# The place of the down projections in the first feed-forward block of a hybrid decoder layer

## Chip, cores and metric

The kernel runs on one core of one Trainium2 chip. The metric is the device time of one execution in microseconds (us). Three timed runs of the kernel before gave 2674.72, 2677.0 and 2678.22 us, with a median of 2677.0 us. The profile is of one further execution, which took 2671.87 us.

## The reference

One layer of a decoder: a mixer, a memory cross-attention and a gated convolutional feed-forward part, over 2048 prompt rows and 32 sample rows of 1024 features, in float32. The change lies in the feed-forward part alone:

```python
n3 = rmsnorm(x, p['g_ffn'])
g, ffn_state = causal_dwconv(n3 @ p['w_ffn_gate'], ffn_prev, p['w_ffn_conv'], p['b_ffn_conv'])
x = x + (jax.nn.gelu(g) * (n3 @ p['w_ffn_up'])) @ p['w_ffn_down']
```

The hidden width is 3072, which is 24 units of 128 features.

## The kernel before

Phases 0 to 2 hold the mixer and the cross-attention. Phase 3 (`phase3`, L668) is the feed-forward part. It takes the 2080 columns (rows of x) in three blocks of 696, 692 and 692 columns; the change touches the first. In each block a hand-written plan (L692 to L700) sets the order of the program: 24 gate/up units `g` and 12 down projections `d`, each `d` for a pair of units. In the first block of the kernel before, pair c (units 2c and 2c+1) has its down projection right behind unit 2c+2; the last two pairs have theirs behind unit 23.

A gate/up unit (`gate_up`, L1353) computes a gate and an up matrix product of one unit as seven products of half size, from combinations of weights and inputs. Each product has 4 steps of 3 matmuls (every float32 number is split into a high and a low part), 12 matmuls of 348 columns, so 84 in a unit. The products go to four PSUM banks: X takes products 0 and 4, Y product 1, Z products 2 and 5, V products 3 and 6. VectorE (DVE) adds Y to `u`, then Z and V to what came of that. The product behind each bank's second use waits for the first use to be read: product 5 for the add of Z, product 6 for the add that writes `up[:, H:W]` from V (H is 348, half of the block). Behind product 5 comes the add into `gb`, and behind product 6 the add into the other half of `up`. Then the tail of the unit runs on ScalarE (ACT) and DVE: `gc` (L1404 on ACT, two L1406 on DVE, the gelu L1407 on ACT), the product into `up` (L1408), and the split of `up` into its high part `ah` (ACT, L79) and its low part `al` (DVE, L83).

A down projection (`down`, L1418) has eight groups, one for each 128 output features. A group is 12 matmuls, six of the pair's first unit and six of the second, into a PSUM tile `pd` of which there are two. Behind each group DVE adds `pd` into `acc` (L1430). Group m+2 waits until the add of group m has freed its tile.

Weights come in pieces (`piece`, L659): seven for a unit, four for a down projection. Raw weights `wr` are loaded by DMA on the queue of SyncE (SP) into four slots, two for each unit or down projection. ACT writes the high half of a piece `pc`, GpSimd (POOL) or DVE the low half (L79, L83). In the first block DVE also makes four sums of raw weights for each unit (`ws`, L606), and the pieces made of them are written to DRAM (`kept_s`), from which the other two blocks load them. Pieces are asked for four ahead of their use, and there are six slots for them. POOL, ACT and DVE also prepare the next block's inputs beside this (L761, L766, L774).

The tile framework decides the order of each engine's queue at build time, by the program's order as priority and by its own estimate of when an operation becomes ready. Each queue then runs in that order. Slots matter here: `ah` and `al` have four slots each (2·CH), `up` and `gc` one, the temporaries `u`, `u2`, `u4` three.

```python
up = q1.tile([128, W], F, name="up")
ah = q1.tile([128, W], R, name="ah", bufs=2 * CH)
```

Of the kernel before, what the change touches and what calls it, by code (L numbers as in the profile page):

```python
# [23 lines left out]
CH = 2  # L24
SMQ, SMO = 1, 2
OUT_PRIO = 170
N3_PRIO = 400
X0_PRIO = 100
G_MIX, G_CROSS, G_MEM, G_FFN, G_FIN = 0, 8, 16, 24, 32
C_CW, C_CB, C_BA, C_BX, C_LAM = 40, 56, 60, 64, 68  # L30
C_FW, C_FB, C_SINK, C_SROW, C_END = 72, 144, 168, 176, 177
# [14 lines left out]
class _Kernel:  # L46
# [295 lines left out]
    def p1_load(self, s, k):  # L342
        t0, W = SB1[s][0], self.width1(s)
        if s == 0:
            if k not in self.x0:
                self.x0[k] = self.lp.tile([128, W], F, name="x0", tag=f"lru{k % 2}", bufs=4)
                with self.tc.high_priority(X0_PRIO):
                    self.nc.sync.dma_start(self.x0[k], self.I["x"][k, :, t0:t0 + W])
# [233 lines left out]
    def piece_stream(self):  # L582

        nc, I = self.nc, self.I
        kept = {}

        def load(src):
            raw = self.wraw.tile([128, 1024], F, name="wr", tag="wr")  # L590
            nc.sync.dma_start(raw, src)
            return raw

        def raws(kind, i):
            if kind == "d":
                return [load(I["w_down"][i * CH + e]) for e in range(CH)]
            g = load(I["w_gate"][i])
            if ("s", i, 0) not in kept:
                return g, load(I["w_up"][i])
            u = self.wsum.tile([128, 512], F, name="ws", tag="ws")  # L600
            nc.sync.dma_start(u, I["w_up"][i][:, 512:1024])
            return g, u

        def sums(x, y, op):
            t = self.wsum.tile([128, 512], F, name="ws", tag="ws")
            nc.vector.tensor_tensor(out=t, in0=x, in1=y, op=op)  # L606
            return t

        def halves(src, lo_eng):
            t = self.wpc.tile([128, 2, 512], R, name="pc", tag="pc")  # L610
            self.split(src, t[:, 0], t[:, 1], "act", lo_eng)
            return t

        def keep(key, src, lo_eng="dve"):
            t = halves(src, lo_eng)
            kept[key] = self.dram.tile([128, 2, 512], F, name="kept_" + "_".join(map(str, key)))
            nc.sync.dma_start(kept[key], t.bitcast(F))
            return t

        def again(key):  # L620
            t = self.wpc.tile([128, 2, 512], R, name="pc", tag="pc")
            nc.sync.dma_start(t.bitcast(F), kept[key])
            return t

        def paired(f, g, u):
            a11, a12 = g[:, 0:512], g[:, 512:1024]
            if ("s", f, 0) in kept:
                yield halves(a11, "pool")
                for e in range(3):
                    yield again(("s", f, e))  # L630
                yield halves(a12, "pool")
                yield again(("s", f, 3))
                yield halves(u, "pool")
                return
            a21, a22 = u[:, 0:512], u[:, 512:1024]
            yield halves(a11, "pool")
            s1 = sums(a21, a22, OP.add)
            s2 = sums(s1, a11, OP.subtract)
            yield keep(("s", f, 0), s2)
            yield keep(("s", f, 1), s1, "pool")  # L640
            yield keep(("s", f, 2), sums(a11, a21, OP.subtract))
            yield halves(a12, "pool")
            yield keep(("s", f, 3), sums(a12, s2, OP.subtract))
            yield halves(a22, "pool")

        def plain(rs):
            for h in range(2):
                for r in rs:
                    yield halves(r[:, h * 512:h * 512 + 512], "pool")

        nxt = raws(*self.units[0])
        for n, (kind, i) in enumerate(self.units):
            now, nxt = nxt, None
            for t in paired(i, *now) if kind == "g" else plain(now):
                yield t
                if nxt is None and n + 1 < len(self.units):
                    nxt = raws(*self.units[n + 1])

    def piece(self, ahead=4):  # L659
        while len(self.pq) <= ahead:  # L660
# [7 lines left out]
    def phase3(self):  # L668
        nc, tc, I, O = self.nc, self.tc, self.I, self.O
        NC = NF // CH  # L670
        with ExitStack() as es:
            pool = lambda n, b: es.enter_context(self.tc.tile_pool(name=n, bufs=b))
            self.wpc = pool("wpc", 6)
            self.wsum = pool("wsum", 3)
            self.n3a = pool("n3a", 1)
            self.n3b = pool("n3b", 1)
            self.q1 = pool("f1", 1)
            self.q2 = pool("f2", 2)
            self.xs = es.enter_context(tc.tile_pool(name="x3", bufs=1, side="right"))
            self.psa = es.enter_context(tc.tile_pool(name="ps3a", bufs=1, space=bass.MemoryType.PSUM))  # L680
            self.psb = es.enter_context(tc.tile_pool(name="ps3b", bufs=1, space=bass.MemoryType.PSUM))
            self.pq = []
            self.p3c = []
            self.n3 = {}
            with tc.high_priority(N3_PRIO):
                for i in range(7):
                    self.p3_ops(0, i)
            self.xpool = lambda: dict(pool=self.xs, tag="x", bufs=4)
            self.fst = self.q1.tile([128, NF, NB, 2], F, name="fst")
            nc.sync.dma_start(self.fst, I["ffn_conv"])  # L690
            self.sfo = self.q1.tile([128, NF, NB, 2], F, name="sfo")
            plan = []  # L692
            for s in range(3):
                for f in range(NF):
                    plan.append(("g", s, f))
                    c = f // CH - 1
                    if f % CH == 0 and f and not (s < 2 and c == NC - 2):
                        plan.append(("d", s, c))
                if s < 2:
                    plan += [("d", s, NC - 2), ("d", s, NC - 1)]  # L700
            self.units = [(k, i) for k, s, i in plan if k in "gd"] + [("d", NC - 1)]
            self.pieces = self.piece_stream()
            acts, sb = {}, None
            for kind, s, i in plan:
                if kind == "g":
                    if i == 0:
                        rest = sb.final() if s else self.p2[3].rstd3_steps()
                        ready = self.p3_prep(s + 1) if s < 2 else iter(())
                        sb = _P3(self, s)

                    def after(e, s=s, i=i):
                        if i < 2 and (s or i) and not (i == 0 and e in (0, 1, 3, 4)):
                            next(rest, None)
                            if i == 1 and e > 3:
                                next(rest, None)
                        elif 4 <= i < 20 and e % 3 == 1:
                            next(ready, None)
                        if s < 2 and i == NF - 1:
                            self.p3_ops(s + 1, e)

                    acts[i] = sb.gate_up(i, after)
                    if i == 1:
                        sb.load_acc()
                else:
                    sb.down([acts[i * CH + e] for e in range(CH)], s < 2 and i == NC - 1)
            sb.tail([acts[NF - CH + e] for e in range(CH)])
# [897 lines left out]
```

## Time and profile before

| | us |
|---|---|
| median of three timed runs | 2677.0 |
| lowest and highest of them | 2674.72, 2678.22 |
| the profiled execution | 2671.87 |
| its span, first to last instruction | 2670.1 |
| TensorE busy in the span | 2567.0 (96%) |
| DVE busy in the span | 1547.3 (58%) |

The profile is one execution. TensorE appears as PE (matmuls) and PEld (weight loads), the granted TensorE clock as a share of full speed. Times in rows count from the span's start. An idle time in brackets is the one just before the instruction, with what ended it. In the views by stretch each engine has its busy time and its number of instructions.

### The profile page before, as it was taken

The numbers are of one execution on the slowest core, as the hardware profiler recorded it, in microseconds if no ns is written. First come the engines' busy times: TensorE is split into PE (matmuls) and PEld (weight loads), VectorE is DVE, ScalarE is ACT, GpSimd is POOL, SyncE is SP. The second block draws the span as 40 slices with busy tenths as digits, with TensorE's granted clock in tenths as the row PEclk, the third lists the DMA queues.
The fourth block names the chain that finished last, engine by engine and source line by source line (L and its number), as shares of the span: only waits on it lengthen the run. The fifth ranks groups of instructions, "written<-read, shape, count | busy, mean of one in ns | idle before, by whom it ended". The sixth has DMA issues, their size and how long they took to land.

```text
span 2670.1 us, 40945 instructions
## 1 busy us (share of the span) xinstructions
PE 2567.0 (96%) x15221; PEld 2408.2 (90%) x15221; DVE 1547.3 (58%) x2637; ACT 1078.8 (40%) x2071; POOL 992.6 (37%) x928
## 2 busy tenths in 40 slices
PE   6999999998999999899999999999999999999997
PEld 5778788986998887899999999999999999999997
DVE  6577666666542434677777675554544454454545
ACT  5455736474442434434343443232332333233233
POOL 3422211013302144445454545453543444343342
PEclk9899999999999999999999999999999999999998
DMA  7664544466756787955555668665564875545442
GB/s 248 249 225 171 192 148 148 151 214 235 271 174 231 246 273 266 348 182 210 177 212 182 213 233 307 206 204 205 197 207 166 302 255 173 159 160 167 148 164 78
DMA packets 195671, 553.72 MB, mean 207 GB/s; under 512 B 28628, under 2 KB 49364, under 8 KB 192784
## 3 DMA queue, kind: packets, MB, share of 16 engines
q1 hardware_dynamic: 195472, 551.10, 59.7%
q8 instruction: 120, 1.97, 0.3%
q14 instruction: 79, 0.65, 0.1%
HBM read 409.22 MB, written 141.80 MB: 206 GB/s over the span
## 4 chain that ended last, share of the span: by engine, by line
PE 78%; DVE 8%; DMA 5%; ACT 3%; issue 3%; POOL 2%; SPq 0%; POOLq 0%; DVEq 0%; ACTq 0%
PE pg L137 30%; PE pd L137 19%; PE pin L137 10%; PE po L137 6%; PE pmo L137 3%; PE pq L137 3%; DVE gc L1406 2%; PE sc L137 1%; DVE ws L606 1%; DMA wr<-in_w_up_dram 1%; PE tp L859 1%; DMA x<-in_x_dram 1%; PE pa L137 1%; DMA x<-x2d 1%; PE msc L137 1%
## 5 line engine op out<-in xcount | busy, mean ns | idle before, releaser
L137 PE MATMUL pg<-n,pc 128*128 128x346 f32 (+1 forms) x6048 | 977.6, 322 | 7.4 <-DVE up L1360 3.1
L137 PEld LDWEIGHTS pg<-n,pc 128*128 128x128 f32 x6048 | 968.6, 189 | 10.8 <-issue 3.8
L83 POOL TENSOR_TENSOR pc<-wr,pc 128x512 fp32r<-128x512 f32 x312 | 435.6, 1403 | 374.9 <-ACT pc L79 372.0
L137 PE MATMUL pd<-ah,pc 128*128 128x346 f32 (+1 forms) x2240 | 461.8, 325 | 22.7 <-DVE acc L1430 22.7
L137 PEld LDWEIGHTS pd<-ah,pc 128*128 128x128 f32 x2240 | 378.8, 191 | 26.8 <-DVE acc L1430 25.5
L79 ACT ACTIVATE pc<-wr 128x512 fp32r<-128x512 f32 x312 | 195.2, 628 | 412.2 <-PE pd L137 255.6
L1430 DVE TENSOR_TENSOR acc<-pd,acc 128x692 f32<-128x692 f32 (+1 forms) x280 | 245.4, 877 | 163.8 <-PE pd L137 162.2
L137 PE MATMUL pd<-al,pc 128*128 128x346 f32 (+1 forms) x1120 | 271.7, 324 | 0.0
L1406 DVE SCALAR_TENSOR_TENSOR gc<-gb,pp,gc 128x696 f32<-128x696 f32 (+2 forms) x144 | 156.5, 1087 | 79.0 <-ACT gc L1404 77.4
L137 PEld LDWEIGHTS pd<-al,pc 128*128 128x128 f32 x1120 | 197.1, 191 | 0.0
L137 PE MATMUL pin<-n1h,wh 128*128 128x512 f32 (+1 forms) x560 | 187.7, 362 | 4.0 <-DVE ql L83 1.7
L137 PE MATMUL pin<-n1l,wh 128*128 128x512 f32 (+1 forms) x560 | 186.0, 358 | 4.7 <-DVE n1l L83 4.7
L137 PE MATMUL pin<-n1h,wl 128*128 128x512 f32 (+1 forms) x560 | 185.2, 357 | 1.7 <-POOL wl L83 1.7
L83 POOL TENSOR_TENSOR wl<-wr,wh 128x1024 fp32r<-128x1024 f32 x35 | 85.6, 2454 | 208.9 <-ACT wh L79 162.1
L1360 DVE TENSOR_TENSOR u<-pg,u 128x346 f32<-128x346 f32 (+1 forms) x144 | 73.9, 513 | 127.5 <-PE pg L137 127.5
L83 POOL TENSOR_TENSOR pc<-ws,pc 128x512 fp32r<-128x512 f32 x72 | 97.8, 1359 | 129.8 <-ACT pc L79 116.8
L1360 DVE TENSOR_TENSOR gb<-pg,u 128x314 f32<-128x314 f32 (+2 forms) x96 | 38.8, 425 | 161.3 <-PE pg L137 161.3
L137 PEld LDWEIGHTS pin<-n1h,wh 128*128 128x128 f32 x560 | 103.2, 194 | 21.3 <-DVE ql L83 2.3
L79 ACT ACTIVATE pc<-ws 128x512 fp32r<-128x512 f32 x144 | 89.8, 626 | 78.9 <-PE pd L137 25.8
L137 PEld LDWEIGHTS pin<-n1l,wh 128*128 128x128 f32 x560 | 102.5, 193 | 19.8 <-DVE n1l L83 5.8
L137 PEld LDWEIGHTS pin<-n1h,wl 128*128 128x128 f32 x560 | 102.7, 194 | 16.9 <-POOL wl L83 2.1
L766 POOL TENSOR_TENSOR n3s<-x,n3s 128x346 fp32r<-128x346 f32 (+1 forms) x72 | 73.4, 1022 | 84.1 <-ACT n3s L765 84.1
(317 smaller groups left out, 4230.3 us busy)
## 6 DMA issues: line engine op xcount, KB each, us to landing
pc<-kept_s SPq DMA_DIRECT2D x192, 512.0 KB, 4.4
kept_s<-pc SPq DMA_DIRECT2D x96, 512.0 KB, 4.1
wh<-keeph SPq DMA_DIRECT2D x90, 512.0 KB, 3.9
wl<-keepl SPq DMA_DIRECT2D x90, 512.0 KB, 5.0
wr<-in_w_gate_dram SPq DMA_DIRECT2D x72, 512.0 KB, 4.2
wr<-in_w_down_dram SPq DMA_DIRECT2D x72, 512.0 KB, 4.0
opd<-n3s SPq DMA_DIRECT2D x56, 346.0 KB, 2.9
n<-opd SPq DMA_DIRECT2D x14, 1384.0 KB, 13.0
```

The source lines that it names most:

```text
L79: nc.scalar.activation(hi, src, AF.Copy)
L83: return e.tensor_tensor(out=lo, in0=src, in1=hi.bitcast(F), op=OP.subtract).ins
L137: nc.tensor.matmul(o, w[a], xs, start=first and n == 0, stop=last and n == 2, skip_group_check=more)
L606: nc.vector.tensor_tensor(out=t, in0=x, in1=y, op=op)
L766: after("pool", nc.gpsimd.tensor_tensor(out=t[:, 1], in0=src, in1=t[:, 0].bitcast(F), op=OP.subtract))
L859: nc.tensor.transpose(tp[:, j], st[:, j, c * 128:(c + 1) * 128], K.ident)
L1360: mark["dve"] = nc.vector.tensor_tensor(out=o, in0=p, in1=t, op=OP.add).ins
L1406: nc.vector.scalar_tensor_tensor(gc, gb[:, k:k + NW], K.col(C_FW, 24 * k + f), gc, op0=OP.mult, op1=OP.add)
L1430: nc.vector.tensor_tensor(out=v, in0=pd[:, :, 0:H], in1=v, op=OP.add)
```

## The change

Pair c's down projection (c from 0 to 9) leaves its place behind unit 2c+2 of the first block. It is issued inside unit 2c+5, between that unit's fifth product (product 4) and its sixth. The last two pairs stay behind unit 23. The order of pieces and of raw weight loads follows: in such a unit the down projection's raw weights are asked for after the first piece, its four pieces come behind the fifth, and the next unit's raw weights are asked for with the seventh piece. No instruction is added or removed, and no tile or number of slots changes. Blocks 2 and 3 keep their order.

```diff
+DOWN_AT = 5
...
-        nxt = raws(*self.units[0])
-        for n, (kind, i) in enumerate(self.units):
-            now, nxt = nxt, None
-            for t in paired(i, *now) if kind == "g" else plain(now):
-                yield t
-                if nxt is None and n + 1 < len(self.units):
-                    nxt = raws(*self.units[n + 1])
+        def order():
+
+            units = iter(self.units)
+            nxt = raws(*next(units))
+            for kind, i, inner in self.uses:
+                now, nxt = nxt, None
+                got = 0
+                for t in paired(i, *now) if kind == "g" else plain(now):
+                    got += 1
+                    if inner is None:
+                        yield t
+                        if nxt is None:
+                            n = next(units, None)
+                            nxt = n and raws(*n)
+                        continue
+                    if got == 7:
+                        n = next(units, None)
+                        nxt = n and raws(*n)
+                    yield t
+                    if got == 1:
+                        down = raws(*next(units))
+                    if got == DOWN_AT:
+                        yield from plain(down)
+
+        yield from order()
...
-                    if f % CH == 0 and f and not (s < 2 and c == NC - 2):
+                    if s and f % CH == 0 and f and not (s < 2 and c == NC - 2):
                         plan.append(("d", s, c))
+                    if not s and f % CH and 0 < c < NC - 1:
+                        inner[f] = c - 1
+                        plan.append(("i", s, c - 1))
...
+                        if not s and e == DOWN_AT - 1 and i in inner:
+                            sb.down([acts[inner[i] * CH + a] for a in range(CH)])
```

## Rows read from the trace of the kernel before

**Rows 1.** The page's first part (busy time, share of the span and instructions of each engine), and from its fifth part the group of the additions into `acc`.
```profile
PE 2567.0 (96%) x15221; PEld 2408.2 (90%) x15221; DVE 1547.3 (58%) x2637; ACT 1078.8 (40%) x2071; POOL 992.6 (37%) x928
...
L1430 DVE TENSOR_TENSOR acc<-pd,acc 128x692 f32<-128x692 f32 (+1 forms) x280 | 245.4, 877 | 163.8 <-PE pd L137 162.2
```

**Rows 2.** Busy time by stretch: the first ten down projections of the first block, each from its first matmul to the next unit's first (the rows 15 to 23 us wide); among them some stretches of two units (27 to 30 us); then the last three units (40.2 us), the last two down projections (30.6 us) and 420 us of the second block. Columns: stretch, its width, busy time (instructions) of PE, PEld, DVE, ACT, POOL, granted clock, DMA share, GB/s.
```profile
1126.50:1141.80 15.30, 15.30 (x98) 15.30 (x97) 11.64 (x15) 2.32 (x4) 2.61 (x4) 1.00 0.68 255
1141.80:1169.00 27.20, 27.05 (x170) 26.77 (x169) 23.14 (x29) 14.84 (x26) 18.17 (x15) 1.00 0.67 245
1169.00:1191.50 22.50, 17.92 (x98) 17.63 (x97) 16.78 (x20) 4.95 (x7) 7.78 (x7) 0.85 0.33 117
...
1218.30:1236.30 18.00, 15.54 (x98) 15.25 (x97) 14.60 (x19) 4.96 (x7) 4.40 (x5) 1.00 0.40 146
1236.30:1266.70 30.40, 27.98 (x171) 27.73 (x170) 20.33 (x25) 13.65 (x24) 20.68 (x18) 0.97 0.65 228
1266.70:1283.60 16.90, 16.25 (x98) 15.96 (x98) 13.38 (x18) 4.96 (x7) 2.82 (x4) 0.96 0.35 132
...
1310.40:1329.00 18.60, 15.51 (x98) 15.23 (x97) 15.21 (x19) 4.96 (x7) 3.96 (x5) 1.00 0.39 142
...
1356.40:1376.50 20.10, 17.15 (x98) 16.87 (x98) 15.15 (x19) 4.96 (x7) 6.16 (x7) 0.92 0.35 131
1376.50:1403.30 26.80, 26.80 (x169) 26.80 (x169) 17.43 (x22) 13.93 (x25) 18.12 (x17) 1.00 0.67 230
1403.30:1421.30 18.00, 15.57 (x98) 15.28 (x98) 14.55 (x19) 4.96 (x7) 4.36 (x6) 1.00 0.40 147
...
1448.70:1468.70 20.00, 17.05 (x97) 16.76 (x96) 15.09 (x19) 4.96 (x7) 6.09 (x6) 0.91 0.38 132
...
1495.50:1513.50 18.00, 15.56 (x98) 15.28 (x97) 14.59 (x19) 4.96 (x7) 4.38 (x5) 1.00 0.40 147
...
1540.30:1557.10 16.80, 15.61 (x98) 15.32 (x97) 13.31 (x18) 4.96 (x7) 2.82 (x4) 1.00 0.33 126
1557.10:1597.30 40.20, 40.20 (x254) 40.20 (x253) 25.58 (x37) 20.85 (x34) 21.86 (x20) 1.00 0.76 270
1597.30:1627.90 30.60, 30.60 (x194) 30.60 (x193) 17.21 (x20) 9.21 (x14) 13.27 (x11) 1.00 0.85 348
...
1680.00:2100.00 420.00, 420.00 (x2624) 418.63 (x2622) 208.33 (x265) 136.16 (x228) 194.40 (x184) 1.00 0.58 197
```

**Rows 3.** Who waited for whom from 1141 to 1557 us (total, times, longest).
```profile
PE pd L137 <- DVE acc L1430: 22.7, 9, 4.6
...
DVE ws L606 <- DMA wr<-in_w_up_dram: 16.0, 9, 3.7
...
PE pg L137 <- DVE up L1360: 3.1, 3, 2.4
```

**Rows 4.** PE in order of time around one down projection: two units, the first two groups, the third group's start. Columns: start, duration, engine, line, operation, count, idle time before.
```profile
1376.48 26.98 PE L137 MATMUL pg<-n,pc 128*128 128x348 f32 x168
1403.30 0.48 PE L137 MATMUL pd<-ah,pc 128*128 128x348 f32 x2
...
1406.80 0.48 PE L137 MATMUL pd<-ah,pc 128*128 128x348 f32 x2
1409.71 0.59 PE L137 MATMUL pd<-ah,pc 128*128 128x348 f32 x2 [2.43 <-DVE acc L1430]
```

**Rows 5.** DVE in order of time over the end of those units and the start of that down projection.
```profile
1397.74 0.52 DVE L1360 TENSOR_TENSOR up<-pg,u 128x348 f32<-128x348 f32 x1 [0.61 <-PE pg L137]
1399.62 0.69 DVE L606 TENSOR_TENSOR ws<-wr 128x512 f32<-128x512 f32 x1 [1.36 <-DMA wr<-in_w_up_dram]
1400.35 1.66 DVE L606 TENSOR_TENSOR ws<-ws,wr 128x512 f32<-128x512 f32 x1
1401.93 1.78 DVE L606 TENSOR_TENSOR ws<-wr 128x512 f32<-128x512 f32 x1
1403.63 0.51 DVE L1360 TENSOR_TENSOR gb<-pg,u 128x348 f32<-128x348 f32 x1
1405.24 1.74 DVE L1406 SCALAR_TENSOR_TENSOR gc<-gb,pp,gc 128x696 f32<-128x696 f32 x1 [1.10 <-ACT gc L1404]
1406.90 0.51 DVE L1360 TENSOR_TENSOR up<-pg,u 128x348 f32<-128x348 f32 x1
1407.33 0.93 DVE L1406 SCALAR_TENSOR_TENSOR gc<-gb,pp,gc 128x696 f32<-128x696 f32 x1
1408.18 0.68 DVE L83 TENSOR_TENSOR pc<-ws,pc 128x512 fp32r<-128x512 f32 x1
1408.79 0.87 DVE L1430 TENSOR_TENSOR acc<-pd,acc 128x696 f32<-128x696 f32 x1
```

**Rows 6.** POOL in order of time beside that.
```profile
1399.71 5.15 POOL L83 TENSOR_TENSOR pc<-wr,pc 128x512 fp32r<-128x512 f32 x3
```

**Rows 7.** The instructions on `ah`, `al` and on `acc` from 1141 to 1557 us: count, duration in ns (shortest/median/longest), first and last start.
```profile
L79 ACT ACTIVATE ah<-up x18: 767/778/789, 1161.5 to 1546.3; 128x696 fp32r<-128x696 f32 x18
L83 DVE TENSOR_TENSOR al<-up,ah x18: 882/1165/1955, 1163.1 to 1547.1; 128x696 fp32r<-128x696 f32 x18
...
L1430 DVE TENSOR_TENSOR acc<-pd,acc x72: 868/876/884, 1142.1 to 1555.4; 128x696 f32<-128x696 f32 x72
```

**Rows 8.** DVE right behind the end of the down projection that ends at 1376.48 us: the last addition.
```profile
1376.68 0.88 DVE L1430 TENSOR_TENSOR acc<-pd,acc 128x696 f32<-128x696 f32 x1 [1.04 <-PE pd L137]
```

**Rows 9.** The instructions on `wr` from 1141 to 1557 us: the sums on DVE with their durations in ns, POOL's low halves of raw weights, and the time from issue to landing of the loads.
```profile
L83 POOL TENSOR_TENSOR pc<-wr,pc x90: 1262/1297/1939, 1144.7 to 1540.7; 128x512 fp32r<-128x512 f32 x90
L606 DVE TENSOR_TENSOR ws<-wr x38: 674/692/1778, 1141.5 to 1552.6; 128x512 f32<-128x512 f32 x38
...
DMA to landing us min/median/max: 3.1/4.0/6.0
```

More of the change, by code (lines that the diff above doesn't have):

```diff
@@ L691, in phase3 @@
             self.sfo = self.q1.tile([128, NF, NB, 2], F, name="sfo")
-            plan = []
+            plan, inner = [], {}
             for s in range(3):
@@ L696, in phase3 @@
                     c = f // CH - 1
-                    if f % CH == 0 and f and not (s < 2 and c == NC - 2):
+                    if s and f % CH == 0 and f and not (s < 2 and c == NC - 2):
                         plan.append(("d", s, c))
+                    if not s and f % CH and 0 < c < NC - 1:
+                        inner[f] = c - 1
+                        plan.append(("i", s, c - 1))
                 if s < 2:
                     plan += [("d", s, NC - 2), ("d", s, NC - 1)]
-            self.units = [(k, i) for k, s, i in plan if k in "gd"] + [("d", NC - 1)]
+            self.units = [(k if k == "g" else "d", i) for k, s, i in plan] + [("d", NC - 1)]
+            self.uses = [(k, i, inner.get(i) if k == "g" and not s else None) for k, s, i in plan if k != "i"]
+            self.uses.append(("d", NC - 1, None))
+            plan = [p for p in plan if p[0] != "i"]
             self.pieces = self.piece_stream()
```

## The prediction

> **What bounds the kernel now.** I read the page's busy shares first. TensorE is busy for 2567.0 of 2670.1 us, and no other engine above 58% [rows 1]. So only what makes TensorE wait, or runs it at its lower clock, is worth anything. Next I read the first feed-forward block by stretch [rows 2]. A down projection without a wait takes 15.3 us (the first of the block, and the last two with 30.6), two units take 26.8. The second block has 420.0 us of matmul in 420 us, so nothing is to be had there. In the first block nine of the ten down projections that the change moves are longer: 22.5, 18.0, 16.9, 18.6, 20.1, 18.0, 20.0, 18.0 and 16.8 us. Their sum is 168.9, less 9 x 15.3 = 137.7, which leaves **31.2 us**. That is what the change can address. The waits name the cause: nine waits of a down projection for the addition into `acc` on DVE, 22.7 us [rows 3]. The other 8.5 us lie mostly in stretches whose granted clock is 0.85, 0.91, 0.92 or 0.96, that is partly at 1.2 instead of 2.4 GHz, each time in a stretch in which TensorE had waited [rows 2].
>
> Then I read where DVE is at that time. The units end at 1403.30 and two groups of the down projection run; the third waits 2.43 us until 1409.71 [rows 4]. The addition of the first group starts at 1408.79 only [rows 5]. The first group had ended 12 matmuls after 1403.30, at about 1405.2 (a matmul of 348 columns takes 26.8 / 168 = 0.16 us), so DVE is 3.6 us late. Its queue shows why. At 1398.3 it is idle and waits 1.36 us for raw weights; then come three sums of 0.69, 1.66 and 1.78 us, the late add into `gb`, the tail of the unit (`gc` twice) and only then `acc`. So DVE isn't saturated: it is on average 17.4 us busy in 26.8 us of units [rows 2]. It is late because a burst of sums and the tail of the unit meet the start of the down projection. The additions have little slack: a group takes 1.92 us and an addition 0.88 [rows 7], so an addition may be 1.04 us late before TensorE waits.
>
> **The change, part by part.** Nothing is added or removed: the same matmuls, additions, pieces and loads, so every busy time stays. What moves is the place of ten down projections.
>
> *The stall removed.* The down projection now starts 5 x 1.92 = 9.6 us into a unit. The preceding unit's tail is over by then: in the rows the add into `gb` is at 1403.63 and the second `gc` ends at 1408.26, 4.6 us later, and the product and the split of `up` behind it are of that size or wait anyway (below). Behind the fifth product only ACT has to read a bank. The four pieces made ahead of it belong to the down projection, and their low halves are POOL's, not DVE's. Just where the change puts it, behind a second unit's fifth product, the trace of before has DVE idle (the 1.36 us at 1398.3 [rows 5]; 1389.9 + 9.6 is 1399.5). I take the 31.2 us as gone, less what the next two items give back. The first down projection, without a wait now, gains nothing.
>
> *Sums inside the down projection.* The next unit's raw weights now take the slots of the down projection's raw weights, which POOL frees near the fifth product, so they land about 4.0 us later (3.1 to 6.0, [rows 9]), some 3 us into the down projection. The three sums then run between additions. Alone a sum takes 0.69 us and fits in the 1.04 us between two additions; with a late load DVE waits up to 3.7 us [rows 3] with an addition queued behind it, and TensorE loses that less 1.04, at most 2.7 us. Bounds: 0 to 2.7 us for each of ten. The waits for loads are 16.0 us in nine, mean 1.8, so a typical one costs 0.7 and not every one meets an addition: I take 0.5 each, **5 us**.
>
> *A new wait ahead of the seventh product.* Five pairs' units are now made before the first down projection, and `ah` and `al` have four slots. So unit 2c+4 can split `up` only when the down projection inside unit 2c+5 has read unit 2c. Until then `up`, which has one slot, isn't free, so the add that writes `up[:, H:W]` of unit 2c+5 from V waits, and the seventh product waits for V. Worked from the down projection's end: the last read of `ah` of unit 2c is six matmuls earlier, -0.96. A consumer starts 0.20 behind TensorE's end [rows 8], so ACT starts at -0.76 and is done at +0.02 (0.778, [rows 7]); `al` ends at +0.95 (0.88 alone, first in DVE's queue), the add (0.52) at +1.5. TensorE has the sixth product to do until +1.92: no wait. If the last addition into `acc` goes first (0.88) and `al` takes its median, 1.165, V is free at 0.20 + 0.88 + 1.17 + 0.52 = 2.77: a wait of 0.85. With `al` at its longest, 1.955, it is 1.65. Bounds 0 to 1.65 for each of ten; I take the middle of the first two, 0.4, and 0.1 for ACT's other work: **5 us**. Queued behind the waiting split on ACT and `al` on DVE are halves of later pieces, which are four ahead of their use; the queues' order is fixed by estimated readiness, so these two should stand behind the additions, not ahead of them.
>
> *What lengthens `al`.* The sums take 1.66 and 1.78 us just while POOL runs three low halves in 5.15 us [rows 5, 6] (1.30 each at the median [rows 9]), and `al` ranges from 0.88 to 1.96, while the 72 additions into `acc`, with one input in PSUM, all took 0.868 to 0.884 [rows 7]. The Trainium skill, page "SBUF — State Buffer", section "Who interferes with whom", has the rule: a DVE instruction with two SBUF inputs and a GpSimd instruction that reads SBUF exclude each other, and the second waits for the whole of the first; one with a single SBUF input is free of that. By that rule the trace agrees for `acc`. It speaks against this change, which makes `al`, with two SBUF inputs, part of what TensorE waits for: with POOL's 1.30 ahead of `al` each time (2.18 in all) the two orders above would give waits of 0.8 and 1.9 us, 14 us for ten instead of 5, and 2665 us, which lies inside the forecast's spread.
>
> *Other queues.* SP's queue: the raw loads are issued in another order but as many, and load time is covered by four pieces of lead, 7.7 us in a down projection. The loads of the next block's inputs behind unit 23's products start earlier by up to 15.3 us. I take zero for both; if that cover failed, one wait of the longest load, 6.0 us [rows 9], stands at a block's edge. The excess in the stretches of units (3.6 us in the stretch from 1236.30, 0.4 from 1141.80, [rows 2]; the waits there are for `up` on DVE, [rows 3]) I leave as it is.
>
> **Sum.** 31.2 - 5 - 5 = 21.2 us. The profiled execution takes 2671.87 us (span 2670.1 and 1.8 around it), so it would take 2650.7; it lies 5.1 below the median of the three runs, which gives 2677.0 - 21.2 = **2655.8**, and I say 2656. With both new costs at zero it is 2677.0 - 31.2 = 2645.8, and about 2642 if the 3.6 us go too. With the middle wait at 0.85 and the sums at 1.0 each it is 2677 - 31.2 + 18.5 = 2664; with both at their ends (27 + 16.5 = 43.5) it would be 12 us slower than now.
>
> About 0.2% (5.4 us) is what a measurement of this kernel can tell from no change.
>
> **Rivals.**
> 1. *The new wait takes over: slower.* If in DVE's fixed order the next unit's sums stand ahead of `al`, V comes free behind a load's wait and three slow sums. As at 1398.3 to 1403.6, that is 1.36 + 0.69 + 1.66 + 1.78 = 5.5 us before `al`, so V is free at about 0.05 + 5.5 + 1.17 + 0.52 = 7.2 and the seventh product waits 5.3. Ten of them are 53 us, and waits of that length were followed by lower clock (a wait of 4.6, the longest, and a granted clock of 0.85 in the down projection that took 22.5, 7.2 too long, so up to 2.6 more each [rows 2, 3]). Net 2677 - 31.2 + 53 = 2699, to 2725 with the clock. It decides from a new wait of 3.1 us for each pair. For it: `up` has one slot, and DVE did run sums ahead of urgent work [rows 5]. Against: the raw weights should land before the middle of the down projection, so the sums should be done before its end. Chance 0.12.
> 2. *The stall only changes its place: same.* If DVE meets late loads in the middle of the down projection and TensorE waits twice the mean, and `al` is slow each time (2 x 0.75 + 1.65 = 3.1 for each of ten), 31 us come back: 2672 to 2682. For it: the sums and their loads now fall in the stretch with least slack. Chance 0.11.
> 3. *The change doesn't do what it says: same.* The framework sets each queue by readiness; had it estimated the down projection's groups to be late, it could put the sixth product and the next unit's first between them, and DVE's collision would stay: 2677 give or take 5. The waits of before show that its estimate didn't foresee DVE's lateness, so I give it 0.03.
>
> **How the numbers follow.** Forecast 0.74 (2640 to 2671), rivals 0.12, 0.11 and 0.03. Predicted is the forecast's 2656. Faster by over 0.2% is 0.74, within 0.2% is 0.14 and slower by over 0.2% is 0.12. The range leaves out the slower rival (0.12) and some 0.06 below and at the upper edge: 2641 to 2680.
>
> **What would show it.** Right: in the first block's moved down projections, stretches near 15.3 us, waits of `pd` for `acc` well under 22.7 us in all, and granted clock near 1.00 from 1126 us on. The new item shows as waits of `pg` for `up` on DVE in the odd units, each ahead of 12 matmuls, under 1 us; blocks 2 and 3 unchanged. Wrong: such waits above 3 us, DVE's sums standing between the last addition and `al`, or TensorE's waits for pieces at the units behind a moved down projection.

## The result, and the profile after

The changed kernel takes 2707.46 us (median of four runs, 2703.98 to 2710.8), the kernel before 2675.86 beside it (2674.31 to 2678.22): a ratio of 1.0121, with a 95% interval of 1.0106 to 1.0137. It is slower by 32 us where a time 21 us shorter had been forecast. The profiled execution has a span of 2705.4 us, 35.3 more than before.

By stretch, the ten moved down projections of the first block, one stretch of two units between them, and 420 us of the second block (columns as in [rows 2]):

```profile
1166.80:1187.20 20.40, 17.52 (x99) 16.54 (x98) 10.25 (x14) 5.86 (x12) 12.05 (x11) 0.92 0.66 245
1214.50:1238.30 23.80, 17.10 (x98) 16.81 (x97) 10.03 (x12) 3.01 (x6) 5.86 (x5) 0.86 0.47 156
1267.00:1289.50 22.50, 17.02 (x99) 16.74 (x98) 9.64 (x13) 4.00 (x9) 7.57 (x6) 0.92 0.44 148
1316.80:1340.50 23.70, 17.29 (x99) 17.00 (x98) 10.03 (x12) 3.02 (x6) 5.86 (x5) 0.86 0.47 156
1340.50:1369.20 28.70, 27.40 (x169) 26.73 (x169) 25.40 (x30) 13.65 (x26) 18.84 (x17) 1.00 0.48 178
1369.20:1391.70 22.50, 17.11 (x98) 16.82 (x97) 9.63 (x13) 3.95 (x9) 7.58 (x6) 0.85 0.42 148
...
1419.00:1442.80 23.80, 17.30 (x98) 17.02 (x97) 10.05 (x12) 2.98 (x6) 5.87 (x5) 0.86 0.47 156
1471.60:1494.20 22.60, 17.03 (x98) 16.74 (x97) 9.58 (x13) 3.92 (x8) 7.52 (x6) 0.85 0.44 148
1521.50:1542.00 20.50, 17.24 (x99) 16.95 (x98) 10.54 (x12) 3.07 (x6) 5.86 (x5) 0.92 0.42 146
1569.10:1585.60 16.50, 15.49 (x97) 15.20 (x96) 9.42 (x11) 2.99 (x6) 2.59 (x2) 1.00 0.45 147
1612.80:1628.10 15.30, 15.30 (x97) 15.30 (x96) 6.18 (x7) 2.36 (x4) 2.59 (x2) 1.00 1.00 423
1715.00:2135.00 420.00, 420.00 (x2622) 418.42 (x2621) 208.42 (x265) 136.26 (x228) 193.35 (x184) 1.00 0.58 195
```

The ten sum to 211.6 us, 58.6 more than ten of 15.3, where before there were 31.2 more [rows 2]: 27 of the 35 us lie here. The second block is as full as before. Three details matter. DVE is now busy for some 10 us in these stretches where it was 15, so it isn't overloaded; and the last two, inside units 21 and 23, take 1.2 us and 0 too much. The first (20.4 us, 15.3 before) has a cause of its own, a wait for a piece of its weights:

```profile
1170.49 1.53 PE L138 MATMUL pd<-ah,pc 128*128 128x348 f32 x4 [2.86 <-POOL pc L84]
```

The lower clock, 0.85 or 0.86 of full speed where the waits are longest, follows them as before: TensorE's busy time in the ten stretches sums to 168.4 us, 15.4 more than ten of 15.3.

PE's waits over the block's moved part, 1186 to 1521 us, and DVE's for raw weights (total, times, longest; compare [rows 3]):

```profile
PE pd L138 <- DVE acc L1457: 36.0, 6, 6.7
PE pg L138 <- DVE gb L1387: 2.8, 3, 0.9
PE pg L138 <- DVE up L1387: 1.9, 7, 0.4
```

```profile
DVE ws L607 <- DMA wr<-in_w_up_dram: 33.6, 6, 6.6
```

TensorE loses 36.0 us in six waits of the third group, and DVE waits 33.6 us in six for raw weights: the same six places. One of them, in order of time on DVE, then on SP's queue, then on POOL (the down projection starts at 1316.83):

```profile
1316.32 1.76 DVE L84 TENSOR_TENSOR pc<-ws,pc 128x512 fp32r<-128x512 f32 x1 [0.91 <-ACT pc L80]
1324.37 0.69 DVE L607 TENSOR_TENSOR ws<-wr 128x512 f32<-128x512 f32 x1 [6.29 <-DMA wr<-in_w_up_dram]
1325.10 0.69 DVE L607 TENSOR_TENSOR ws<-ws,wr 128x512 f32<-128x512 f32 x1
1325.70 0.69 DVE L607 TENSOR_TENSOR ws<-wr 128x512 f32<-128x512 f32 x1
1326.31 1.67 DVE L1457 TENSOR_TENSOR acc<-pd,acc 128x696 f32<-128x696 f32 x2
```

```profile
1310.01 0.33 SPq L592 DMA_DIRECT2D wr<-in_w_gate_dram  x1
1315.04 0.32 SPq L794 DMA_DIRECT2D opd<-n3s  x1
1315.45 0.48 SPq L759 DMA_DIRECT2D x<-x2d  x1
1318.90 0.32 SPq L794 DMA_DIRECT2D opd<-n3s  x1
1319.27 0.42 SPq L592 DMA_DIRECT2D wr<-in_w_up_dram  x1
```

```profile
1314.97 2.56 POOL L84 TENSOR_TENSOR pc<-wr,pc 128x512 fp32r<-128x512 f32 x2
1317.49 1.39 POOL L793 TENSOR_TENSOR n3s<-x,n3s 128x346 fp32r<-128x346 f32 x1
```

To read it: the first two groups have ended at 1316.83 + 3.84 = 1320.7, and their additions run only at 1326.31, because three sums stand ahead of them in DVE's queue and the first of these waits for the up weights of the next unit. That load was issued at 1319.27, 2.44 us behind the start of the down projection. A raw slot had come free with POOL's low halves of the down projection's own pieces, done at 1317.53; then the load stood in SP's queue behind a store of the next block's inputs that waited for POOL's work at 1317.49 (until 1318.88).

That holds for every second of the six. In the others no store is in the way. Beside the down projection that starts at 1369.21, on POOL and then on SP's queue:

```profile
1369.09 3.05 POOL L84 TENSOR_TENSOR pc<-wr,pc 128x512 fp32r<-128x512 f32 x2
```

```profile
1372.17 0.33 SPq L592 DMA_DIRECT2D wr<-in_w_up_dram  x1
```

The load goes as soon as POOL's two low halves are done (1372.14), 2.96 us behind the start: here the slot alone makes it late.

### The profile page after: what moved, and what is told of

It reads as the page before. It is cut to its first block, busy times and chain, and to the rows that moved or that the text cites. A ratio compares the mean times of both kernels' runs of the same rounds, so it can differ in the third digit from the quotient of the medians.

```text
span 2705.4 us, 40876 instructions
## 1 busy us (share of the span) xinstructions
PE 2577.6 (95%) x15221; PEld 2413.6 (89%) x15221; DVE 1556.9 (58%) x2637; ACT 1073.4 (40%) x2071; POOL 1009.3 (37%) x928
## 4 chain that ended last, share of the span: by engine, by line
PE 43%; DVE 4%; POOL 2%; DMA 2%; issue 1%; ACT 1%; POOLq 0%; SPq 0%; ACTq 0%; DVEq 0%
PE pg L138 25%; PE pd L138 17%; POOL pc L84 1%; DMA wr<-in_w_up_dram 1%; DVE ws L607 1%; DVE gc L1433 1%; DMA wr<-in_w_down_dram 1%; POOL n3s L793 0%; PE pt L138 0%; DVE acc L1457 0%; DVE pc L84 0%; ACT gc L1431 0%; DVE up L1387 0%; POOL x L788 0%; DVE al L84 0%
## 5 line engine op out<-in xcount | busy, mean ns | idle before, releaser
L138 PE MATMUL pd<-ah,pc 128*128 128x346 f32 (+1 forms) x2240 | 467.1, 328 | 43.4 <-DVE acc L1457 40.3
L793 POOL TENSOR_TENSOR n3s<-x,n3s 128x346 fp32r<-128x346 f32 (+1 forms) x72 | 80.1, 1116 | 77.3 <-ACT n3s L792 75.2
```

The source lines that it names most:

```text
L138: nc.tensor.matmul(o, w[a], xs, start=first and n == 0, stop=last and n == 2, skip_group_check=more)
L793: after("pool", nc.gpsimd.tensor_tensor(out=t[:, 1], in0=src, in1=t[:, 0].bitcast(F), op=OP.subtract))
```

## The experiments

Theory A: the order of DVE's queue. The three sums for the next unit stand ahead of the first addition and wait there for a late load. Theory B: the slots of `ah`, `al` and `up`, filled one pair longer, hold DVE and ACT back. All medians stand beside those of the kernel before on the same chip.

**The order alone.** Two kernels, the changed one and the one before, got the same edit, a manual order on DVE without any wait of its own:

```diff
-            nc.vector.tensor_tensor(out=t, in0=x, in1=y, op=op)
+            self.behind(nc.vector.tensor_tensor(out=t, in0=x, in1=y, op=op), self.mark.get("acc"), "sums order")
...
-            nc.vector.tensor_tensor(out=v, in0=pd[:, :, 0:H], in1=v, op=OP.add)
+            K.mark["acc"] = nc.vector.tensor_tensor(out=v, in0=pd[:, :, 0:H], in1=v, op=OP.add).ins
```

> The changed kernel with one more order: each sum of raw weights on DVE stands behind the last addition into acc that the program has issued before it. Theory A (DVE's order: in most moved down projections the three sums for the next unit stand ahead of the first addition and wait there for a late raw load, 33.6 us in six of them): the waits of the down projections for the additions, 40.3 us in the changed kernel, fall below 8 us, each moved down projection takes 15.3 to 16.5 us, and with the lower clock gone the time falls by 45 to 55 us, to 2652 to 2662. Theory B (the four slots of ah and al and the one of up, filled one pair longer, hold DVE and ACT back): nothing changes, 2702 to 2712.

Measured: 2659.35 us, ratio 0.9931 (0.9916 to 0.9946). In the kernel of this run there is no wait of `pd` for `acc` left. One down projection in order of time on DVE (it starts at 1306.64):

```profile
1308.76 0.88 DVE L1457 TENSOR_TENSOR acc<-pd,acc 128x696 f32<-128x696 f32 x1 [1.78 <-PE pd L138]
1310.68 0.88 DVE L1457 TENSOR_TENSOR acc<-pd,acc 128x696 f32<-128x696 f32 x1 [1.04 <-PE pd L138]
1312.60 0.88 DVE L1457 TENSOR_TENSOR acc<-pd,acc 128x696 f32<-128x696 f32 x1 [1.04 <-PE pd L138]
1314.52 0.88 DVE L1457 TENSOR_TENSOR acc<-pd,acc 128x696 f32<-128x696 f32 x1 [1.04 <-PE pd L138]
1315.32 0.83 DVE L607 TENSOR_TENSOR ws<-wr 128x512 f32<-128x512 f32 x1
1316.19 0.69 DVE L607 TENSOR_TENSOR ws<-ws,wr 128x512 f32<-128x512 f32 x1
```

Each addition now waits for TensorE and not the other way round. The raw load is still late against the down projection (issued at 1308.18, 1.54 us behind its start), and it costs nothing, since nothing urgent stands behind the waiting instruction. Theory A holds, B falls. The first moved down projection, which waits for its pieces, still takes 22.4 us.

> The kernel before with the same order for its sums. There two of the three sums are issued ahead of the down projection's additions and stay where they are, the third moves behind the fourth addition. Theory A: one sum (up to 1.78 us) less ahead of the tail of the unit, so each wait of 2.4 to 3.1 us becomes 0.7 to 1.5; the waits fall from 22.7 to about 10 us and the time by 10 to 18 us, to 2658 to 2666. Theory B: the kernel before has no such slot wait and its waits come from the tail alone, so it stays within 4 us of 2676.

Measured: 2659.99 us, 0.9931 (0.9908 to 0.9953). The time is as expected; the waits for the additions went from 22.7 to 14.1 us, not to about 10. So the kernel before had the same fault in a milder form: moving one of its three sums took off 16 us.

**All three sums, in the kernel before.** The sums that are issued while a down projection is issued are collected and set behind its fourth addition:

```diff
-            nc.vector.tensor_tensor(out=t, in0=x, in1=y, op=op)
+            self.late.append(nc.vector.tensor_tensor(out=t, in0=x, in1=y, op=op))
...
+            if m == 0:
+                K.late = []
...
+            add = nc.vector.tensor_tensor(out=v, in0=pd[:, :, 0:H], in1=v, op=OP.add)
+            if m == 3:
+                for t in K.late:
+                    K.behind(t, add.ins, "sums order")
```

> The kernel before with all three sums that are issued during a down projection set behind that down projection's fourth addition. Theory A for the kernel before (its waits come from the sums ahead of the tail): waits for the additions under 5 us and 2645 to 2657. Rival (the unit's tail alone delays the first addition past the third group): waits of about 1.4 us each remain as with one sum moved, 2657 to 2664.

Measured: 2651.03 us, 0.99 (0.9885 to 0.9915), the lowest median of all. PE's waits in its first block:

```profile
PE pd L137 <- DVE acc L1433: 7.0, 11, 0.7
```

The waits are 7.0 where under 5 was expected, each 0.7 us or less. What is left stands mostly ahead of the eighth group. One of these waits on PE, and DVE ahead of it:

```profile
1317.36 0.58 PE L137 MATMUL pd<-ah,pc 128*128 128x348 f32 x2 [0.74 <-DVE acc L1433]
```

```profile
1313.34 0.88 DVE L1433 TENSOR_TENSOR acc<-pd,acc 128x696 f32<-128x696 f32 x1
1314.13 2.38 DVE L83 TENSOR_TENSOR pc<-ws,pc 128x512 fp32r<-128x512 f32 x2
1316.44 0.87 DVE L1433 TENSOR_TENSOR acc<-pd,acc 128x696 f32<-128x696 f32 x1
```

The sixth addition stands behind two low halves made of the sums just moved: the burst comes later and costs less, it isn't gone. The edit also let the framework put two matmuls of the next unit among the last groups, so TensorE's order isn't quite that of the kernel before. The time is as expected. So with its sums out of the way the old place needs no mid-unit move.

**The sums' data instead of their order.** The sums read weights that are loaded earlier, so this kernel no longer computes the layer and serves for its times alone:

```diff
-            s1 = sums(a21, a22, OP.add)
+            s1 = sums(a11, a12, OP.add)
...
-            yield keep(("s", f, 2), sums(a11, a21, OP.subtract))
+            yield keep(("s", f, 2), sums(a11, a12, OP.subtract))
```

> The changed kernel with the three sums made of the two halves of the gate weights, whose load is issued some 9 us earlier, in place of the up weights: what is computed is another product, and the same number of sums stands at the same kind of place in DVE's queue. Theory A (the sums hurt because they wait there for a late load): DVE's wait for raw loads falls from 33.6 us to under 8, the waits for the additions from 40.3 to under 10, 2655 to 2672. Rival A3 (three sums ahead of the additions hurt by their own length, 2 to 5 us, whenever the load lands): waits of 2 us or more remain in most down projections, 2680 to 2700.

Measured: 2668.43 us, 0.9956 (0.9942 to 0.9971). DVE's waits for raw loads from 1186 to 1521 us, and PE's for the additions in the block:

```profile
DVE ws L607 <- DMA wr<-in_w_gate_dram: 3.7, 4, 1.6
```

```profile
PE pd L138 <- DVE acc L1457: 8.3, 6, 1.9
```

The sums cost little when their load has landed. Six waits of 1.9 us or less are left and 39 us of the time are back: the late load is most of the price, not the sums' own length (rival A3 expected 2680 to 2700). Some of it remains: the ten moved down projections take 17.5 us more than ten of 15.3 here, against 58.6 in the changed kernel and 7 with the order alone.

**Why the load is late.** Two kernels change SP's queue. In the first the stores of the prepared inputs go to POOL's queue:

```diff
-            nc.sync.dma_start(self.opd[s][BUDDY.index(nm)][:, 2 * k:2 * k + 2], t.bitcast(F))
+            nc.gpsimd.dma_start(self.opd[s][BUDDY.index(nm)][:, 2 * k:2 * k + 2], t.bitcast(F))
```

> The changed kernel with the stores of the next block's prepared inputs (opd) issued from POOL's queue, not SP's. Theory A in its full form (the raw load for the sums, which itself waits for nothing, is late because it stands in SP's queue behind stores that wait up to 6.0 us for POOL): the load is issued about 4 us earlier, DVE's waits for raw loads fall from 33.6 us to under 15 and the time by 15 to 30 us, to 2677 to 2692, less what POOL pays for issuing. Rival A2 (the load is late because its slot is freed late): the waits stay at 30 us or more and the time within 5 us of 2707.

Measured: 2756.06 us, 1.0292 (1.0273 to 1.0311), slower by 49 us than the changed kernel. DVE's waits from 1186 to 1521 us and POOL's cost of issuing:

```profile
DVE ws L607 <- DMA wr<-in_w_up_dram: 13.9, 7, 2.6
```

```profile
L794 POOL DMA_DIRECT2D opd<-n3s x84 | 47.1, 561 | 19.6 <-POOL n3s L793 14.5 <-PE pg L138 4.2 <-DMA opd<-n3s 0.9
```

DVE's waits for the load fell from 33.6 to 13.9 us, as expected, but that overstates it: TensorE's waits for the additions fell only from 36.0 to 28.5 us in the same window. Two neighbouring moved down projections, which start at 1341.04 and 1389.95, on SP's queue and on PE:

```profile
1340.93 0.33 SPq L592 DMA_DIRECT2D wr<-in_w_up_dram  x1
...
1393.30 0.33 SPq L592 DMA_DIRECT2D wr<-in_w_up_dram  x1
```

```profile
1347.93 0.59 PE L138 MATMUL pd<-ah,pc 128*128 128x348 f32 x2 [2.89 <-DVE acc L1457]
...
1400.26 0.95 PE L138 MATMUL pd<-ah,pc 128*128 128x348 f32 x2 [5.67 <-DVE acc L1457]
```

Where the store had stood in the way, the load goes 0.11 us ahead of the start and the wait is 2.9 us in place of some 6.5. In the others it goes 3.35 behind, no earlier than before, and the wait of 5.7 is as long as before (5.4); DVE waits less for the load there only because it gets to it later, behind a low half that took 3.69 us. So theory A in its full form is right for every second one and rival A2 for the rest. The forecast of the time was wrong: the profiled execution has 46.6 us more of span than that of the changed kernel, 36 of them outside the first block. POOL has 84 issues of 561 ns, 47.1 us in all, in the preparation of all three blocks; that they are what costs the time is argued, not shown (POOL's busy time in all grew by 20.2 us, from 1009.3).

In the second the preparation is only issued one product later:

```diff
-                        elif 4 <= i < 20 and e % 3 == 1:
+                        elif 4 <= i < 20 and e % 3 == (1 if s else 2):
```

> The changed kernel with the preparation of the next block's inputs one product later in each unit of the first block (behind products 2 and 5 in place of 1 and 4), so that one store less stands in SP's queue ahead of the raw load for the sums. Theory A with the late load made by SP's queue: the load is issued 1.5 to 4 us earlier, the waits of 5.4 to 6.7 us become 2 to 4, and the time is 2672 to 2692. Rival A2 (its slot is freed late): waits of 5 us or more, 2700 to 2712.

Measured: 2695.84 us, 1.0066 (1.0051 to 1.0081), between the two theories. One down projection (start at 1316.12) on SP's queue and on DVE:

```profile
1314.69 0.32 SPq L794 DMA_DIRECT2D opd<-n3s  x1
1315.95 0.33 SPq L592 DMA_DIRECT2D wr<-in_w_up_dram  x1
```

```profile
1319.53 0.79 DVE L607 TENSOR_TENSOR ws<-wr 128x512 f32<-128x512 f32 x1 [3.06 <-DMA wr<-in_w_up_dram]
```

One store less ahead of it, and the load goes 0.17 us ahead of the down projection's start in place of 2.44 behind. Every second wait of TensorE shrank to 2.4 us (the first of these to 3.1), the others stayed at 5.0 (5.4 to 5.6 in the changed kernel), with a load 2.92 us behind the start as before. They are the same ones as in the run above: the store on SP makes the load late in every second moved down projection, and the slot that POOL frees late in the rest. The ninth agrees in the changed kernel: it lies inside unit 21, where no preparation is issued any more, and had 1.2 us too much. The tenth says nothing here, since no sums stand among its additions. An order that puts the store behind the load was not run.

**One odd unit earlier.** The slot theory by itself: pair c inside unit 2c+3.

```diff
-                    if not s and f % CH and 0 < c < NC - 1:
-                        inner[f] = c - 1
-                        plan.append(("i", s, c - 1))
+                    if not s and f % CH and 0 <= c < NC - 1:
+                        inner[f] = c
+                        plan.append(("i", s, c))
...
-                    plan += [("d", s, NC - 2), ("d", s, NC - 1)]
+                    plan += [("d", s, c) for c in ((NC - 2, NC - 1) if s else (NC - 1,))]
```

> The changed kernel with each down projection one odd unit earlier: pair c inside unit 2c+3, at the same place behind the fifth product, so that a slot of ah and al is free when the next unit's tail wants it. Theory A: the short waits ahead of the sixth and seventh products go (about 5 us in all), the waits for the additions stay near 40 us, since the same sums stand at the same place: 2697 to 2708. Theory B: the waits for the additions go too, 2650 to 2665.

Measured: 2705.02 us, 1.0106 (1.0089 to 1.0123), the time that theory A gave. Its detail was off: the waits for the additions fell to 26.4 us, but waits of products for `u` on DVE, 8.4 us, and one of 5.0 for a piece came in their stead. The last of these is the edge of the block, as in the next run, so the agreement is in part luck.

> Both edits together: pair c inside unit 2c+3, and each sum behind the last addition issued before it. Theory A (DVE's order) with the slots as a small separate cost: the waits for the additions stay gone, and the waits of 0.6 to 1.2 us ahead of the sixth and seventh products, 6.9 us in the changed kernel with the order, go as well, with a part of the first down projection's 3.9: 2645 to 2655. Theory B in the form that is left (the order alone pays and the pair's place doesn't matter): 2657 to 2662.

Measured: 2668.35 us, 0.9966 (0.9954 to 0.9977), 9 us slower than the order alone and outside both expectations. The trace has this at the end of the block:

```profile
1603.58 0.58 PE L138 MATMUL pg<-n,pc 128*128 128x346 f32 x2
1609.36 3.25 PE L138 MATMUL pg<-n,pc 128*128 128x346 f32 x10 [5.20 <-POOL pc L84]
```

Products of 346 columns are the second block's: the framework had put its first product into the last down projection of the first block, where it waited for a piece. The next kernel leaves the last two pairs where the changed kernel has them (`0 <= c < NC - 2`, and the plan's last line unchanged):

> As the kernel with both edits (pair c inside unit 2c+3, sums behind the additions), but with the last two pairs left behind unit 23 as in the changed kernel, so that the end of the block is issued as before. That kernel took 2668.35 us, and its trace shows the next block's first product in the middle of the last down projection, waiting 5.2 us for a piece from POOL. If that reordering at the block's edge is why it missed 2645 to 2655, the wait goes with its lower clock: 2654 to 2662, about the time of the changed kernel with the order alone (2659.35). If not (the waits of 0.4 to 1.35 us ahead of products, 9.3 us, were the reason), it stays at 2665 to 2671.

Measured: 2654.08 us, 0.9919 (0.9901 to 0.9938): the edge was the main reason. In the profiles the block is some 10 us shorter than with both edits, 5.2 of them that wait. Against the order alone the median is 5.3 us lower. The profiles of these two differ by 6.8 us of span: 3.2 ahead of the block (first product at 1073.08 here, at 1076.23 there) and 5.0 in it, less 1.4 behind it. Some 2 of the 5.0 are a lower clock there in units ahead of the first moved down projection, so the earlier pair itself is worth some 3 us at most. The place in a unit brings nothing that was shown: this kernel and the old place with all three sums moved (0.99, 0.9885 to 0.9915) are not told apart.

## Why the prediction was wrong, step by step

*What bounds the kernel.* Right: 33.7 of the 35.3 us lie between the first product of the first block and that of the second (554.9 us before, 588.6 after), 27.4 of them in the moved down projections, and waits of TensorE with the lower clock behind them made these.

*The stall removed, 31.2 us.* The mechanism was half right. A down projection in the middle of a unit does escape the unit's tail: with the order edit the moved ones take 15.3 to 15.4 us from the second on. But the prediction read the cause as a burst of sums and the tail together, and took the burst as gone by the move. Moving one or all of the three sums, with the old place kept, gave 16 and 27 us. The sums were the part that mattered. The prediction also took the 1.36 us at 1398.3 for room on DVE, just where the change puts the down projection. They were the first sum's wait for its load [rows 5]: an engine that waits in its queue is idle and yet not free. And the first down projection, which was to gain nothing, lost 5.1 us to a wait for its pieces and the lower clock behind it.

*Sums inside the down projection, 5 us (0 to 27).* **This is the step that failed.** It said that the sums run between additions, and that a late load costs TensorE at most 3.7 - 1.04 = 2.7 us. In the changed kernel they stand ahead of the first addition in eight of the ten, and the wait was 5.4 to 6.7 us in six of ten and 3.3 in a seventh: 40.3 us with their eighth in all. With the slower matmuls behind the waits the term of 5 us came to 53.5 us (58.6 less the first one's 5.1), and the down projections' excess rose by 27.4 where it should have fallen by 26. Two errors lie in it. The bound of 3.7 came from waits of the kernel before, whose load is issued earlier against its use; and the load was put some 3 us into the down projection, where it landed at 7.5 (1324.4 - 1316.8), 5.1 us behind its issue. Both rest on the assumption that SP and POOL hand the slot on at once, while "Other queues" took SP's queue at zero with a cover of four pieces. In fact the load was issued 2.4 to 3.0 us behind the start in these six, by the store or by the slot. The cover exists for the pieces; it doesn't for the sums, which DVE takes up as soon as its queue reaches them.

*The order by estimated readiness.* The prediction used it for `al` ("should stand behind the additions, not ahead of them") and forgot it for the sums. The trace shows the sums ahead of the additions; by the rule of the order the framework must have estimated the load to land in time (its estimate itself isn't on record), and a fixed queue has no way back. The first rival had this mechanism (sums waiting for a load ahead of urgent work in DVE's fixed order) and a time of 2699 to 2725 that holds the result, but named `al` at the end of the down projection as the victim, and gave it 0.12 with the argument that the raw weights land before the middle.

*The new wait ahead of the seventh product, 5 us.* It didn't come. In the stretch from 1340.49 TensorE runs 132 matmuls of units without a wait behind the down projection, PE in order of time:

```profile
1340.49 21.31 PE L138 MATMUL pg<-n,pc 128*128 128x348 f32 x132
1362.73 2.19 PE L138 MATMUL pg<-n,pc 128*128 128x348 f32 x12 [0.92 <-DVE gb L1387]
```

The add that frees V ends at 1342.66, 2.2 us behind the down projection's end. The sixth product covers 1.9 us of that, and two matmuls that the framework put ahead of the seventh cover the rest. Short waits of 0.2 to 0.9 us, 4.7 in all from 1186 to 1521, came later in the units instead, where DVE catches up; they are of the size put down and not at the place.

*The clock.* Left out of the sum as part of the stall. It grew with it: stretches at 0.85 or 0.86 cost about 2 us of slower matmuls each (17.0 to 17.3 us busy against 15.3).

## What to carry to other kernels

Where a framework fixes each engine's queue by estimated readiness, an instruction that waits for a DMA must be asked what stands behind it: its wait is charged to the next urgent work, and moving that work moves the charge. A wait measured at one place is no bound for it at another; follow the load back through its slot and its own queue. If a wait in a trace ends on an engine that isn't busy, try an order on that engine before a new place for the work: here the order alone gave 27 us in the kernel before, the move with an order on the sums 17 to 23.

## What the runs showed of the hardware

All 72 of DVE's additions with one input in PSUM took 0.868 to 0.884 us [rows 7], while sums with two SBUF inputs ranged from 0.67 to 1.78 [rows 9], the long ones beside POOL's low halves [rows 5, 6]. The Trainium skill, page "SBUF — State Buffer", section "Who interferes with whom", has that division, and the trace agrees on which instructions suffer. Issuing a store from POOL's queue took POOL 561 ns each in the run above; the same store from SP's queue took 0.32 us there, and no compute engine has a row for it.
